# Loading v in rows of 16 KiB for sixteen heads at a time, and holding TensorE while both groups of stores are written

## The chip, the cores and the metric

The kernel runs on one core of a Trainium2 chip. The time is that of the whole execution on the device, in microseconds (us). A core has five engines that run side by side and wait for each other by semaphores: TensorE (PE; its weight loads are shown as PEld), VectorE (DVE), ScalarE (ACT), GpSimd (POOL) and SyncE (SP). Sixteen DMA engines move data between the memory outside (HBM) and the core's own memory (SBUF, 128 partitions); transfers are issued by POOL, by SP or by ACT, each with a queue of its own. TensorE writes its results to PSUM, eight banks of 2 KiB for each partition.

## The reference

```python
batch, n_heads, seq, head_dim = 8, 12, 1024, 64
# attn_weights: (8, 12, 1024, 1024) float32, v: (8, 12, 1024, 64) float32

def reference(attn_weights, v):
    return np.einsum('bhqs,bhsd->bhqd', attn_weights, v).astype(np.float32)
```

For each of 96 heads a matrix of 1024 x 1024 is multiplied by one of 1024 x 64. The weights are 403 MB, v and the result 25 MB each.

## The kernel before, in words

**Units.** Heads are taken four at a time, a quad; there are `NV` = 24 of them. A quad is worked in two units, so there are `NU` = 48, counted from 0 here. A partition of SBUF belongs to one of the four heads (32 partitions each) and has 32 rows of that head's weights; a unit has 16 of these rows for each partition. Its load (`load_attn`, L327) is issued by POOL and turns float32 into bfloat16 on the way: 8 MiB are read, 64 KiB in one piece for each partition, and 4 MiB are written to one of the two buffers `abf`. The last two units are loaded in two halves each.

**TensorE.** The loop at L212 has one turn for a quad, with `pe_unit` for each of its units. A unit waits for its load, and transposes it in 16 steps `g` of four matmuls (`transpose_g`, L134); pairs of bfloat16 values are moved as one float32 word. DVE and ACT copy the banks to `at` (L255). Ahead of step 8 TensorE waits for `s_half`, a semaphore that counts units. After the transposes, the first unit of a quad spreads v (`spread_v`, L149), both units transpose the products of the unit before back (`transpose_back`, L161; copied to `osb` by ACT, L238), and then multiply (`multiply`, L176; copied to `ot`, L267).

**v.** v arrives with 32 rows of a head in each partition (8 KiB of float32 in one piece), and is wanted with the rows at other places. `spread_v` does this by matmuls: for each of the four heads, `VB` = 4 matmuls of 32 partitions by 512 columns, with a matrix of ones and zeros (`spread`) as weights, summed in one bank. DVE and ACT copy the four banks to `vbf` (L231). Two quads are loaded together (`load_v`, L333, 2 MiB read), into `vr`, which has a place for each of the two; TensorE's branch at L197 picks the place. The load is issued by POOL when the odd quad of the two before has been spread (a wait for `s_sp`). The first two quads come by SP's queue as float32, in two loads (L124, and L396 in SP's list), to a part of `osb` not in use yet; DVE turns the first to bfloat16 (L312) and POOL the second (L382).

**Order on POOL and SP.** POOL goes through the units: for unit `n` the v load if one is due, then a wait for the last transposes of the unit (`s_t`), then the load of unit `n + 2`, and after units 16 and 32 the stores. Results are gathered in `osb` (ten places): quads 0 to 7 are stored in one DMA of 8 MiB, quads 8 to 15 in two of 2 and 6 MiB (`BURSTS`), the next four by POOL in two of 2 MiB after the last load, and the last four by SP. SP's list hands on semaphores: it waits for a v load and counts up `s_vr` for TensorE; it waits for the first two groups of stores and counts up `s_free` for ACT; it waits for the second halves of the last units and counts up `s_half` (L408). Before that, one increment at the start of the list sets `s_half` to `HALVED` = 46, so only the last two units wait in the middle.

Of the kernel before, what the change touches and what calls it, by code (L numbers as in the profile page):

```python
# [10 lines left out]
def kernel(  # L11
# [18 lines left out]
    nc = tc.nc  # L30
    fp32 = mybir.dt.float32
    bf16 = mybir.dt.bfloat16
    PE, DVE, ACT = (getattr(mybir.EngineType, x) for x in ("PE", "DVE", "Activation"))

    B, H, Q, S = attn_weights.shape
    D = v.shape[-1]
    NH = B * H
    P = 128
    VH = 4
    VP = P // VH  # L40
# [2 lines left out]
    HP = P // 2  # L43
    KW = S // (2 * P)
    SB = S // P
    VB = S // VP // SB
    NV = NH // VH
    NU = 2 * NV

# [1 line left out]
    HELD_FROM = NV - 8  # L51
# [2 lines left out]

    NO = 8 + 2
    V_SLOT = 4

    HALVED = NU - 2
    TOGETHER = 8
    BURSTS = {8: ((0, 8),), 16: ((8, 2), (10, 6))}  # L60

    def slot(q):
        return q % NO
# [5 lines left out]
    def out_n(q, fours):  # L69
# [1 line left out]
            "(n four) (p r) d -> (four p) n (r d)", four=VH, p=VP  # L71
        )

    v_2 = v.rearrange("b h q d -> (b h) q d").rearrange(
        "(hq two four) (p r) d -> hq (four p) two (r d)", two=2, four=VH, p=VP
    )

    def on_dve(g):
        return g % 8 in (0, 2, 4, 5, 7)
# [8 lines left out]
    sem = tc.alloc_semaphore  # L88
    sb = lambda name, shape, dt: nc.alloc_sbuf_tensor(name, shape, dt).ap()
    ident = sb("ident", [P, P], fp32)  # L90
    spread = sb("spread", [P, VB, P], bf16)
    abf = [sb(f"abf{i}", [P, G, S], bf16) for i in range(2)]
    at = sb("at", [P, G, KW, P, 2], bf16)
    vr = sb("vr", [P, 2, VB, SB * D], bf16)
    vbf = sb("vbf", [P, SB, VH, D], bf16)
    ot = sb("ot", [P, GH, P], fp32)
    osb = sb("osb", [P, NO, 2 * G, D], fp32)

    v32 = osb[:, ds(V_SLOT, 2)].rearrange("p n r d -> p n (r d)")
    bank = [nc.alloc_psum_tensor(f"bank{i}", [P, 512], fp32).ap() for i in range(8)]  # L100
    pt = [b.rearrange("p (k j) -> p k j", k=KW) for b in bank[:4]]
    po = bank[4:6]
    px = bank[6:8]
# [1 line left out]

    s_abf = [sem(f"s_abf{i}") for i in range(2)]
    s_second = {n: sem(f"s_second{n}") for n in range(HALVED, NU)}
    s_v0, s_v = sem("s_v0"), sem("s_v")
    s_osb = sem("s_osb")
    s_held, s_end = sem("s_held"), sem("s_end")  # L110

# [8 lines left out]
    s_const, s_vr = sem("s_const"), sem("s_vr")  # L120

    s_half, s_free = sem("s_half"), sem("s_free")

    nc.sync.dma_start(out=v32[:, 0], in_=v_2[0][:, 0])  # L124

    with tc.tile_critical(sync_engine=mybir.EngineType.Pool, no_gpsimd_drain=True):  # L126
        pe = nc.tensor

        def transpose_g(a, g, n):
            if g >= 4:  # L130
                pe.wait_ge(s_cp[g - 4], n)
            words = a[:, g].bitcast(fp32).rearrange("p (c k) -> p k c", k=KW)
            for k in range(KW):
                last = pe.matmul(  # L134
                    out=pt[g % 4][:, k],
                    lhsT=words[:, k],
                    rhs=ident,
                    is_transpose=True,
                    start=(k == 0),
                    stop=(k == KW - 1),  # L140
                )
            last.then_inc(s_t[on_dve(g)])

        def spread_v(two, banks):

            for h, ps in enumerate(banks):
                rows = ds(h * VP, VP)
                for b in range(VB):
                    last = pe.matmul(  # L149
                        out=ps,  # L150
                        lhsT=spread[rows, b],
                        rhs=vr[rows, two, b],
                        start=(b == 0),
                        stop=(b == VB - 1),
                    )
                last.then_inc(s_sp)

        def transpose_back(parts=((0, 4, px[0]), (4, 4, px[1]))):
            for j0, jn, ps in parts:
                for j in range(jn):  # L160
                    last = pe.matmul(  # L161
                        out=ps[:, ds(j * P, P)],
                        lhsT=ot[:, j0 + j],
                        rhs=ident,
                        is_transpose=True,
                        start=(j == 0),
                        stop=(j == jn - 1),
                    )
                last.then_inc(s_back)
# [16 lines left out]
        def pe_unit(i, n, both, loaded, it):  # L186

            pe.wait_ge(*loaded)
            for g in range(G):
                if g == GH:  # L190
                    pe.wait_ge(s_half, n)
                transpose_g(abf[i], g, n)
            pe.wait_ge(s_ot, both)
            if i == 0:
                pe.wait_ge(s_vr, it)
                odd = pe.snap((it - 1) % 2)
                with pe.If(odd > 0):  # L197
                    spread_v(1, po + px)
                with pe.Else():
                    spread_v(0, po + px)  # L200
                pe.wait_ge(s_vbf, it * 4)
            transpose_back()
            pe.wait_ge(s_last, both)
            for hp in range(2):
                for h in range(2):
                    for half in range(2):
                        outs = po[hp][ds(half * D, D), ds(h * GH * VP, GH * VP)]
                        last = multiply(outs, 2 * hp + h, half)
                last.then_inc(s_m)

        pe.wait_ge(s_const, 3 + VH)
        with nc.Fori(1, NV + 1, 1, engines=(PE,)) as it:  # L212
            loaded = pe.snap(it * 16)
            second = pe.snap(it * 2)
# [96 lines left out]
        for half in range(2):  # L311
            last = nc.vector.tensor_copy(  # L312
                out=vr[:, 0, ds(half * (VB // 2), VB // 2)].rearrange("p b x -> p (b x)"),
                in_=v32[:, 0, ds(half * (SB * D * VB // 2), SB * D * VB // 2)],
            )
        last.then_inc(s_vr)
        engine(True)
        engine(False)
        nc.scalar.wait_ge(s_held, 16 * (BY_SYNC - HELD_FROM) // 2)
# [2 lines left out]
        pool = nc.gpsimd  # L322

        def load_attn(n):
            pieces = [(0, G)] if n < HALVED else [(0, GH), (GH, GH)]
            for g0, gn in pieces:
                pool.dma_start(  # L327
                    out=abf[n % 2][:, ds(g0, gn)].rearrange("p g s -> p (g s)"),
                    in_=attn_q[n // 2][:, ds((n % 2 * G + g0) * S, gn * S)],
                ).then_inc(s_abf[n % 2] if g0 == 0 else s_second[n], 16)  # L330

        def load_v(iv):
            pool.dma_start(  # L333
                out=vr.rearrange("p two b x -> p two (b x)"), in_=v_2[iv]
            ).then_inc(s_v, 16)

        def store(q, fours, eng, done):
# [7 lines left out]
        def store_2(q):  # L345
# [7 lines left out]
            out=ident,  # L353
            in_=ident,
            compare_op=mybir.AluOpType.not_equal,
            fill=1.0,
            base=0,
            pattern=[[-1, P]],
            channel_multiplier=1,
        ).then_inc(s_const)  # L360

        for h in range(VH):
            pool.wait_ge(s_const, h + 3)
            pool.affine_select(  # L364
                out=spread[ds(h * VP, VP)],
                in_=spread[ds(h * VP, VP)],
                compare_op=mybir.AluOpType.not_equal,
                fill=1.0,
                base=0,
                pattern=[[1, VB], [-1, P]],  # L370
                channel_multiplier=VB,
            ).then_inc(s_const)
        for n in range(NU - 2):
            q, i = n // 2, n % 2
            if i == 0 and q % 2 == 1 and q + 1 < NV:
                pool.wait_ge(s_sp, 4 * (q + 1))
                load_v((q + 1) // 2)
            pool.wait_ge(s_t[True], (n + 1) * PER_DVE)
            load_attn(n + 2)
            if n == 0:  # L380
                pool.wait_ge(s_v0, 16)
                pool.tensor_copy(  # L382
                    out=vr[:, 1].rearrange("p b x -> p (b x)"), in_=v32[:, 1]
                ).then_inc(s_vr)
            if i == 0 and q % TOGETHER == 0 and 0 < q <= HELD_FROM:
                for q0, fours in BURSTS[q]:
                    store(q0, fours, pool, s_osb)
# [5 lines left out]

        nc.sync.dma_start(out=v32[:, 1], in_=v_2[0][:, 1]).then_inc(s_v0, 16)  # L396
        nc.sync.sem_inc(s_free, NO // 2)
        nc.sync.sem_inc(s_half, HALVED)
        for k in range(1, NV // 2):
            nc.sync.wait_ge(s_v, 16 * k)  # L400
            nc.sync.sem_inc(s_vr, 2)
            stored = 2 * (k - 1)
            if stored % TOGETHER == 0 and 0 < stored <= HELD_FROM:
                nc.sync.wait_ge(s_osb, 16 * sum(len(BURSTS[x]) for x in BURSTS if x <= stored))
                nc.sync.sem_inc(s_free, TOGETHER // 2)
        for n in range(HALVED, NU):
            nc.sync.wait_ge(s_second[n], 16)
            nc.sync.sem_inc(s_half)  # L408
        nc.sync.wait_ge(s_osb, 16 * sum(len(x) for x in BURSTS.values()))
        store(NV - 4, 2, nc.sync, s_end)  # L410
# [4 lines left out]
            out=out_q[NV - 1], in_=osb[:, slot(NV - 1)].rearrange("p r d -> p (r d)")  # L415
# [35 lines left out]
```

## Time and profile before

| What | us |
|---|---|
| median of 3 runs | 1052.8 (1052.76 to 1053.04) |
| the profiled execution | 1052.94 |
| its span, first to last instruction or landing | 1051.2 |
| TensorE busy / its weight loads | 731.1 / 686.2 |
| VectorE / ScalarE / GpSimd busy | 388.2 / 410.3 / 44.6 |
| transposes (L134), 3072 matmuls | 446.8 |
| spreading v (L149), 384 matmuls | 26.1 |
| attention loads, POOL, 46 of 4 MiB in SBUF: issue to landing, median | 30.9 |
| v loads, POOL, 11 of 1 MiB in SBUF: issue to landing, median | 12.5 |
| first v loads, SP, 2 of 1 MiB: issue to landing, median | 14.4 |

"Busy" is the time in which an engine had an instruction of its own under way. A DMA's time from issue to landing holds its stay in the queue behind other transfers. The profile divides the span into 40 slices and gives the busy share of each engine and of the DMA engines in tenths, so that a 9 is a slice that is full.

### The profile page before, as it was taken

To read this page: it belongs to the slowest core of one execution; us is meant where nothing else is said; L and a number is where in the kernel's file an instruction comes from. 1 tells how busy PE (TensorE), PEld (TensorE's weight loads), DVE (VectorE), ACT (ScalarE), POOL (GpSimd) and SP (SyncE) were. 2 spreads that over 40 slices of the span, in tenths; PEclk is the share of its full clock that TensorE was granted. 3 is DMA by queue.
4 is the path that set the end of the run, shared out by engine and by line. 5 is a ranking of instruction groups with operands and counts; after the bars stand their busy time and mean duration, and the time that the engine had idled before them with its cause. 6 is when DMAs were issued, how large, how long until landed. Compare 5 with 4: busy or idle time off the path is not lost.

```text
span 1051.2 us, 16374 instructions
## 1 busy us (share of the span) xinstructions
PE 731.1 (70%) x6920; PEld 686.2 (65%) x6920; DVE 388.2 (37%) x583; ACT 410.3 (39%) x493; POOL 44.6 (4%) x76
## 2 busy tenths in 40 slices
PE   0877688679579576457957858758716875875985
PEld 0767687578478575457857758658716865875874
DVE  1443344335335333233523434335303433532543
ACT  0444345335335333233533434335304433533543
POOL 2000000000000000000000000001000000000000
PEclk9989889889889898688989889889868988988898
DMA  9999999999999999999999999999999999999998
GB/s 233 227 220 217 218 218 208 216 219 219 219 217 218 216 207 379 219 219 217 217 216 208 219 219 219 207 229 217 359 225 219 219 206 229 218 206 218 218 218 343
DMA packets 13685, 240.19 MB, mean 228 GB/s; under 512 B 1136, under 2 KB 1136, under 8 KB 3952
## 3 DMA queue, kind: packets, MB, share of 16 engines
q0 software_dynamic: 12832, 233.84, 99.2%
q1 hardware_dynamic: 848, 6.29, 1.5%
q8 instruction: 2, 0.03, 0.0%
q14 instruction: 3, 0.02, 0.0%
HBM read 427.82 MB, written 25.17 MB: 431 GB/s over the span
## 4 chain that ended last, share of the span: by engine, by line
DMA 78%; PE 20%; issue 1%; POOL 0%; DVE 0%; ACT 0%; POOLq 0%; SPq 0%
DMA abf<-in_attn_weights_dram 78%; PE bank L134 20%; PE bank L176 0%; PE bank L161 0%; POOL abf L327 0%; DVE osb L238 0%; ACT ot L267 0%; SPq L408 0%; POOLq L435 0%; POOLq L126 0%
## 5 line engine op out<-in xcount | busy, mean ns | idle before, releaser
L134 PE MATMUL bank<-ident,abf 128*128 128x128 f32 x3072 | 446.8, 315 | 277.6 <-DMA abf<-in_attn_weights_dram 273.6
L134 PEld LDWEIGHTS bank<-ident,abf 128*128 128x128 f32 x3072 | 437.3, 214 | 290.4 <-DMA abf<-in_attn_weights_dram 285.8
L255 DVE COPY at<-bank 128x1024 bf16<-128x1024 bf16 x480 | 320.4, 689 | 486.8 <-PE bank L134 484.2
L255 ACT COPY at<-bank 128x1024 bf16<-128x1024 bf16 x288 | 288.8, 1012 | 411.9 <-PE bank L134 411.9
L176 PE MATMUL bank<-at,vbf 128*64 128x256 bf16 x3072 | 215.0, 278 | 0.0
L176 PEld LDWEIGHTS bank<-at,vbf 128*64 128x64 bf16 x3072 | 196.7, 108 | 13.4 <-DVE at L255 4.0
L267 ACT COPY ot<-bank 128x512 f32<-128x512 f32 x48 | 28.1, 586 | 174.0 <-PE bank L176 174.0
L267 DVE COPY ot<-bank 128x512 f32<-128x512 f32 x48 | 33.2, 692 | 151.4 <-PE bank L176 151.4
L161 PE MATMUL bank<-ident,ot 128*128 128x128 f32 x392 | 52.2, 276 | 32.5 <-DVE vbf L231 31.9
L161 PEld LDWEIGHTS bank<-ident,ot 128*128 128x128 f32 x392 | 43.4, 141 | 44.6 <-DVE vbf L231 43.7
L238 ACT COPY osb<-bank 128x512 f32 (+1 forms) x97 | 52.1, 589 | 27.3 <-PE bank L161 26.2
L327 POOL DMA_DIRECT2D abf<-in_attn_weights_dram x50 | 27.1, 542 | 716.9 <-PE bank L134 716.0
L231 DVE CAST vbf<-bank 128x512 bf16<-128x512 f32 x48 | 30.9, 686 | 6.5 <-PE bank L149 6.5
L231 ACT CAST vbf<-bank 128x512 bf16<-128x512 f32 x48 | 25.8, 589 | 11.8 <-PE bank L149 11.8
L149 PE MATMUL bank<-vr,spread 32*128 32x512 bf16 x384 | 26.1, 377 | 0.0
L255 ACT ACT_TABLE_LOAD x12 | 15.4, 1283 | 6.1 <-DMA osb<-in_v_dram 5.9
L333 POOL DMA_DIRECT2D vr<-in_v_dram x11 | 7.7, 703 | 228.7 <-PE bank L149 228.7
L149 PEld LDWEIGHTS bank<-vr,spread 32*128 32x128 bf16 x384 | 11.0, 92 | 6.2
L340 POOL DMA_DIRECT2D out_dram<-osb x5 | 3.9, 785 | 6.9 <-ACT osb L238 6.6
L364 POOL TENSOR_SCALAR_AFFINE_SELECT spread<-spread 32x512 bf16<-32x512 bf16 x4 | 3.6, 900 | 0.6
L306 DVE MEMSET ident<- 128x128 f32 x1 | 0.2, 165 | 5.9 <-DMA osb<-in_v_dram 5.9
L382 POOL CAST vr<-osb 128x2048 bf16<-128x2048 f32 x1 | 1.9, 1883 | 0.0
(9 smaller groups left out, 4.3 us busy)
## 6 DMA issues: line engine op xcount, KB each, us to landing
abf<-in_attn_weights_dram POOLq DMA_DIRECT2D x46, 4096.0 KB, 30.9
vr<-in_v_dram POOLq DMA_DIRECT2D x11, 1024.0 KB, 12.5
out_dram<-osb POOLq DMA_DIRECT2D x1, 8192.0 KB, 44.5
abf<-in_attn_weights_dram POOLq DMA_DIRECT2D x4, 2048.0 KB, 24.0
out_dram<-osb POOLq DMA_DIRECT2D x3, 2048.0 KB, 35.8
out_dram<-osb POOLq DMA_DIRECT2D x1, 6144.0 KB, 44.9
osb<-in_v_dram SPq DMA_DIRECT2D x2, 1024.0 KB, 14.4
out_dram<-osb SPq DMA_DIRECT2D x1, 2048.0 KB, 13.9
```

The source lines that it names most:

```text
L134: last = pe.matmul(out=pt[g % 4][:, k], lhsT=words[:, k], rhs=ident, is_transpose=True, start=(k == 0), stop=(k == KW - 1),)
L149: last = pe.matmul(out=ps, lhsT=spread[rows, b], rhs=vr[rows, two, b], start=(b == 0), stop=(b == VB - 1),)
L161: last = pe.matmul(out=ps[:, ds(j * P, P)], lhsT=ot[:, j0 + j], rhs=ident, is_transpose=True, start=(j == 0), stop=(j == jn - 1),)
L176: last = pe.matmul(out=outs, lhsT=vbf[:, 2 * kw + par, h], rhs=at[:, ds(half * GH, GH), kw, ds(h * VP, VP), par], start=(n == 0), stop=(n ...
L231: copy(out=vbf[:, :, h], in_=ps.rearrange("p (k d) -> p k d", k=SB)).then_inc(s_vbf)
L238: return copy(out=rows.rearrange("p (half j) d -> p j half d", half=2)[:, ds(j0, jn)], in_=ps[:, ds(0, jn * P)].rearrange("p (j half d) -> ...
L255: ins = copy(out=at[:, g].rearrange("c k j two -> c (k j two)"), in_=bank[g % 4].bitcast(bf16),)
L267: copy(out=ot.rearrange("c j (h p) -> c h j p", h=VH)[:, ds(2 * e, 2)], in_=po[e].rearrange("c (h j p) -> c h j p", h=2, j=GH),).then_inc( ...
L327: pool.dma_start(out=abf[n % 2][:, ds(g0, gn)].rearrange("p g s -> p (g s)"), in_=attn_q[n // 2][:, ds((n % 2 * G + g0) * S, gn * S)],).th ...
L333: pool.dma_start(out=vr.rearrange("p two b x -> p two (b x)"), in_=v_2[iv]).then_inc(s_v, 16)
L340: eng.dma_start(out=out_n(q, fours), in_=at_slot, **({"single_packet": True} if eng is pool and fours == 2 else {}),).then_inc(done, 16)
L364: pool.affine_select(out=spread[ds(h * VP, VP)], in_=spread[ds(h * VP, VP)], compare_op=mybir.AluOpType.not_equal, fill=1.0, base=0, patte ...
```

## The change

v comes in rows of 16 KiB: a partition holds 64 rows of a head, 16 partitions make a head, and 128 partitions hold eight heads, two quads. `V8` is 8, `VB` (matmuls for each head in `spread_v`) goes from 4 to 8. The two quads of such a load lie in the same place of `vr`, in other partitions; `vr` has two of these places, so four quads. After the first two quads (SP, one load), POOL loads quads 2 and 3 together, and then four quads at a time, at quads 4, 8, 12, 16 and 20 (`V_LOADS`). TensorE's branch picks one of four parts. A matmul of `spread_v` still takes 32 partitions, which now hold parts of two heads; `spread`, written by one select on POOL, has zeros where the other head lies. `spread` is 1080 elements for each partition in place of 512. The conversion of the first two quads is DVE's alone.

`s_half` starts at 18 in place of 46 and is counted up by 16 when the first store has landed and by 12 when both stores of the second group have: so units 18 and 34 wait for these in the middle of their transposes. In SP's list the wait for a group of stores comes ahead of that for a v load.

```diff
-    VB = S // VP // SB
+    V8 = 2 * VH
+    VB = S // (P // V8) // SB
+    VR = 32
...
+    V_AT_ONCE = 4
+    V_LOADS = {2: 2, **{q: V_AT_ONCE for q in range(V_AT_ONCE, NV, V_AT_ONCE)}}
...
+    ENDS = [2 * q + 2 for q in BURSTS] + [HALVED]
+    WHOLE = [n - m for m, n in zip([0] + ENDS, ENDS)]
...
-    v_2 = v.rearrange("b h q d -> (b h) q d").rearrange(
-        "(hq two four) (p r) d -> hq (four p) two (r d)", two=2, four=VH, p=VP
-    )
+    v_h = v.rearrange("b h q d -> (b h) q d")
+
+    def v_n(q, fours):
+        return v_h[ds(q * VH, fours * VH)].rearrange(
+            "(n eight) (p r) d -> (eight p) n (r d)", eight=V8, p=P // V8
+        )
...
-    spread = sb("spread", [P, VB, P], bf16)
+    spread = sb("spread", [P, V8, P + VB - 1], bf16)
...
-    vr = sb("vr", [P, 2, VB, SB * D], bf16)
+    vr = sb("vr", [P, V_AT_ONCE // 2, VB, SB * D], bf16)
...
-    nc.sync.dma_start(out=v32[:, 0], in_=v_2[0][:, 0])
+    nc.sync.dma_start(out=v32, in_=v_n(0, 2)[:, 0])
...
-        def spread_v(two, banks):
+        def spread_v(n, banks):
 
             for h, ps in enumerate(banks):
-                rows = ds(h * VP, VP)
+                j = n % 2 * VH + h
+                rows = ds(j * (P // V8) // VR * VR, VR)
                 for b in range(VB):
                     last = pe.matmul(
                         out=ps,
-                        lhsT=spread[rows, b],
-                        rhs=vr[rows, two, b],
+                        lhsT=spread[rows, j, ds(VB - 1 - b, P)],
+                        rhs=vr[rows, n // 2, b],
...
-                odd = pe.snap((it - 1) % 2)
-                with pe.If(odd > 0):
-                    spread_v(1, po + px)
+                which = pe.snap((it - 1) % V_AT_ONCE)
+                with pe.If(which > 1):
+                    with pe.If(which > 2):
+                        spread_v(3, po + px)
+                    with pe.Else():
+                        spread_v(2, po + px)
                 with pe.Else():
-                    spread_v(0, po + px)
+                    with pe.If(which > 0):
+                        spread_v(1, po + px)
+                    with pe.Else():
+                        spread_v(0, po + px)
...
-        pe.wait_ge(s_const, 3 + VH)
+        pe.wait_ge(s_const, 4)
...
-        def load_v(iv):
+        def load_v(q, fours):
             pool.dma_start(
-                out=vr.rearrange("p two b x -> p two (b x)"), in_=v_2[iv]
+                out=vr[:, ds(q % V_AT_ONCE // 2, fours // 2)].rearrange("p n b x -> p n (b x)"),
+                in_=v_n(q, fours),
             ).then_inc(s_v, 16)
...
-            if i == 0 and q % 2 == 1 and q + 1 < NV:
+            if i == 0 and q + 1 in V_LOADS:
                 pool.wait_ge(s_sp, 4 * (q + 1))
-                load_v((q + 1) // 2)
+                load_v(q + 1, V_LOADS[q + 1])
             pool.wait_ge(s_t[True], (n + 1) * PER_DVE)
             load_attn(n + 2)
-            if n == 0:
-                pool.wait_ge(s_v0, 16)
-                pool.tensor_copy(
-                    out=vr[:, 1].rearrange("p b x -> p (b x)"), in_=v32[:, 1]
-                ).then_inc(s_vr)
...
-        nc.sync.dma_start(out=v32[:, 1], in_=v_2[0][:, 1]).then_inc(s_v0, 16)
         nc.sync.sem_inc(s_free, NO // 2)
-        nc.sync.sem_inc(s_half, HALVED)
+        nc.sync.sem_inc(s_half, WHOLE[0])
         for k in range(1, NV // 2):
-            nc.sync.wait_ge(s_v, 16 * k)
-            nc.sync.sem_inc(s_vr, 2)
             stored = 2 * (k - 1)
-            if stored % TOGETHER == 0 and 0 < stored <= HELD_FROM:
+            if stored in BURSTS:
+                done = list(BURSTS).index(stored)
                 nc.sync.wait_ge(s_osb, 16 * sum(len(BURSTS[x]) for x in BURSTS if x <= stored))
                 nc.sync.sem_inc(s_free, TOGETHER // 2)
+                nc.sync.sem_inc(s_half, WHOLE[done + 1])
+            if 2 * k in V_LOADS:
+                nc.sync.wait_ge(s_v, 16 * (1 + list(V_LOADS).index(2 * k)))
+                nc.sync.sem_inc(s_vr, V_LOADS[2 * k])
```

More of the change, by code (lines that the diff above doesn't have):

```diff
@@ L97 @@
     osb = sb("osb", [P, NO, 2 * G, D], fp32)
-    v32 = osb[:, ds(V_SLOT, 2)].rearrange("p n r d -> p n (r d)")
+    v32 = osb[:, ds(V_SLOT, 2)].rearrange("p n r d -> p (n r d)")
     bank = [nc.alloc_psum_tensor(f"bank{i}", [P, 512], fp32).ap() for i in range(8)]
@@ L107 @@
     s_second = {n: sem(f"s_second{n}") for n in range(HALVED, NU)}
-    s_v0, s_v = sem("s_v0"), sem("s_v")
+    s_v = sem("s_v")
     s_osb = sem("s_osb")
@@ L313 @@
                 out=vr[:, 0, ds(half * (VB // 2), VB // 2)].rearrange("p b x -> p (b x)"),
-                in_=v32[:, 0, ds(half * (SB * D * VB // 2), SB * D * VB // 2)],
+                in_=v32[:, ds(half * (SB * D * VB // 2), SB * D * VB // 2)],
             )
-        last.then_inc(s_vr)
+        last.then_inc(s_vr, 2)
         engine(True)
@@ L360 @@
         ).then_inc(s_const)
[L362 to L372, printed above, removed]
+        pool.wait_ge(s_const, 3)
+        pool.affine_select(
+            out=spread,
+            in_=spread,
+            compare_op=mybir.AluOpType.not_equal,
+            fill=1.0,
+            base=VB - 1,
+            pattern=[[-P, V8], [-1, P + VB - 1]],
+            channel_multiplier=VB,
+        ).then_inc(s_const)
         for n in range(NU - 2):
             q, i = n // 2, n % 2
-            if i == 0 and q % 2 == 1 and q + 1 < NV:
+            if i == 0 and q + 1 in V_LOADS:
                 pool.wait_ge(s_sp, 4 * (q + 1))
-                load_v((q + 1) // 2)
+                load_v(q + 1, V_LOADS[q + 1])
             pool.wait_ge(s_t[True], (n + 1) * PER_DVE)
             load_attn(n + 2)
-            if n == 0:
-                pool.wait_ge(s_v0, 16)
-                pool.tensor_copy(
-                    out=vr[:, 1].rearrange("p b x -> p (b x)"), in_=v32[:, 1]
-                ).then_inc(s_vr)
             if i == 0 and q % TOGETHER == 0 and 0 < q <= HELD_FROM:
```

## The prediction

> **What bounds the kernel now.** I read the slices of the span first, then the DMA queues, the chain of waits and the timeline of TensorE.
>
> ```profile
> PE   0877688679579576457957858758716875875985
> DMA  9999999999999999999999999999999999999998
> q0 software_dynamic: 12832, 233.84, 99.2%
> ```
>
> The DMA row is full in every slice while TensorE's has holes: the sixteen DMA engines set the time. The chain of waits says the same, load after load:
>
> ```profile
> DMA 78%; PE 20%; issue 1%; POOL 0%; DVE 0%; ACT 0%; POOLq 0%; SPq 0%
> 303.97 28.84 DMA abf<-in_attn_weights_dram
> 332.81 0.04 issue
> 332.86 8.03 PE bank L134 x64
> 340.88 0.29 issue
> 341.18 35.21 DMA abf<-in_attn_weights_dram
> ```
>
> Its 20% of TensorE are no bound of their own: while a unit is transposed, the load of the next is under way (35.21 from issue to landing, of which the queue ahead is a good part). The timeline gives prices, because TensorE starts a unit when its load has landed:
>
> ```profile
> 212.02 9.43 PE L134 MATMUL bank<-ident,abf 128*128 128x128 f32 x64 [2.08 <-DMA abf<-in_attn_weights_dram]
> 231.34 10.41 PE L134 MATMUL bank<-ident,abf 128*128 128x128 f32 x64 [4.61 <-DMA abf<-in_attn_weights_dram]
> 250.70 8.02 PE L134 MATMUL bank<-ident,abf 128*128 128x128 f32 x64 [1.10 <-DMA abf<-in_attn_weights_dram]
> 274.88 9.28 PE L134 MATMUL bank<-ident,abf 128*128 128x128 f32 x64 [10.88 <-DMA abf<-in_attn_weights_dram]
> 395.73 10.17 PE L134 MATMUL bank<-ident,abf 128*128 128x128 f32 x64 [4.53 <-DMA abf<-in_attn_weights_dram]
> 434.62 9.63 PE L134 MATMUL bank<-ident,abf 128*128 128x128 f32 x64 [20.88 <-DMA abf<-in_attn_weights_dram]
> ```
>
> Third column: idle before. Landings of plain loads lie 19.32 us apart (231.34 - 212.02), so 8.389 MB move at 434 GB/s. A v load between two makes it 24.18 (274.88 - 250.70), so v costs 4.86; the 8 MiB store makes it 38.89 (434.62 - 395.73), so it costs 19.57.
>
> **The change, part by part.** The sum is made against the profiled execution's 1052.94 us (span 1051.2); the median of the runs is 1052.8, 0.1 lower.
>
> *Rows of v.* One v load is 2.097 MB; at the 434 GB/s of the loads, whose rows are 64 KiB, that is 4.83 us. It costs 4.86, so shorter rows and one more DMA together cost 0.03 to 0.06 (another pair, 332.86 to 357.07, gives 4.89). Eleven loads: 0.3 to 0.7 us. That is all there is to win. Rows twice as long halve the rows' part, and six loads for eleven take away five of eleven DMAs' parts: -0.4 taken, ends 0 and -0.7. A second way of pricing is a rival below.
> The Trainium skill, "DMA: Bandwidth & Descriptors", section on the anatomy of one DMA, has about 2.0 us fixed for each DMA; by it five DMAs less would be an estimated 10 us. The 4.86 above speaks against paying that in a full queue.
>
> *TensorE held.* From unit 18 (start 395.73) the second half of the transposes waits for the first store, from unit 34 for the other two. The store ends where load 19 begins, 434.62 - 19.32 = 415.3. Then 32 transposes, at the half clock that follows such idle time, take 5.6 (as at 1010.60 below), and load 20 goes out near 421.5, before at 408.03. Load 19 is still under way until 434.3, which hides 12.8 us. Behind the held transposes stand only this unit's spread, product and copies; they end near 421.0 + 6.2 + 1.35 + 1.09 + 4.48 = 434.1 (spread as below), when load 19 lands. The second group lies alike. Cost nothing; without that cover 13.5 each. SP waits for the stores ahead of the v loads of later quads: nothing of those is due. For the stores themselves I see no gain: 8.389 MB in 19.57 is the loads' rate already, with TensorE at work beside.
>
> *Start.* SP's one load of 2 MiB replaces two of 1 MiB. DVE, ACT and POOL start with the first's landing, at 5.89. The two took 4.8 (its own view) and, from the median 14.4 of both, 24.0 us; the second ran beside attention's load 0. So the new one lands between 8.3 (2.4 us more bytes) and 29.8; I take 18. DVE then needs 0.17 + 0.57 (a memset of 540 words for 256 in 0.27) before POOL's selects, 0.28 and, at 0.90 per 512 elements, 1.9 for 1080 in one; the casts are 4 of 0.87 instead of 2. All is ready near 24, before load 0 lands at 27.11. At 29.8 TensorE would start 5.6 late (29.8 + 0.17 + 0.57 + 0.28 + 1.9), load 2 would go out at 43.2 for 37.57, and load 1 lands only at 47.66. Nothing either way. POOL's cast (1.88) leaves.
>
> *The spread (L149).*
>
> ```profile
> 323.76 1.07 PE L149 MATMUL bank<-vr,spread 32*128 32x512 bf16 x16
> 325.27 0.70 POOL L333 DMA_DIRECT2D vr<-in_v_dram  x1 [20.77 <-PE bank L149]
> 325.97 0.56 POOL L327 DMA_DIRECT2D abf<-in_attn_weights_dram  x1
> 332.86 1.35 PE L134 MATMUL bank<-ident,abf 128*128 128x128 f32 x9 [1.17 <-DMA abf<-in_attn_weights_dram]
> ```
>
> Sixteen of mean 377 ns end in 1.07 us: four chains side by side, one per group of 32 partitions; in the records matmuls of one group start 0.216 apart. After, it is 32 matmuls, and two heads share a group, so a quad uses two groups, sixteen in each. Two full chains side by side: 15 x 0.216 + 0.38 = 3.6; all in line: 7.1. In L176's records the second half of the columns starts with the fifth matmul of the first half, so about four wait for one part of the array; then the second group starts with the thirteenth of the first: 12 x 0.216 + 3.6 = 6.2. I take 6.2, 5.1 later than now.
> The Trainium skill, "TensorE: Matmul & The Clock Gate", rules for kernel authors, wants each small-K matmul in its own row group and has 3.07 times for four; giving up half of the groups for twice the matmuls is against it: estimated 4 x 1.07 = 4.3 us by its pattern, with the sum as it is.
> Who waits? DVE's and ACT's casts, TensorE's own rest, and in six units POOL: its v load, and the load queued behind it, go out after the spread. The load in flight then lands 7.59 later (332.86 - 325.27); 2.5 remain. Pairs of units take TensorE 9.4 + 6.2 + 1.35 + 1.09 + 4.48 and 9.4 + 1.09 + 4.5 + 0.4 = 37.9, the DMA 38.64 and its share of v: still DMA's. Where it now idles 4.61 its clock halves for a while (10.41 against 8.02); less idle time gives some of it back. Cost in the steady part: nothing as forecast.
>
> *End.*
>
> ```profile
> 1010.60 5.59 PE L134 MATMUL bank<-ident,abf 128*128 128x128 f32 x32 [2.04 <-SPq L408]
> 1016.13 1.07 PE L149 MATMUL bank<-vr,spread 32*128 32x512 bf16 x16
> 1023.97 4.14 PE L134 MATMUL bank<-ident,abf 128*128 128x128 f32 x32
> 1029.98 4.14 PE L134 MATMUL bank<-ident,abf 128*128 128x128 f32 x32 [1.87 <-SPq L408]
> 1041.93 0.33 SPq L414 DMA_DIRECT2D out_dram<-osb  x1
> ```
>
> The last bank is copied 4.6 later, so 1023.97 becomes 1028.6 and the last transposes 1032.7, 2.7 late; the last store goes out at 1044.6. In the DMA view of the end the engines stay full to 1047.4 with the stores queued since 1000.55 and 1030.05; 2.4 us of that is the last store, so it must be there by 1045.0. SP's first packets come 1.0 after issue (0.74, 1.75): 1045.6. Between 0 and +0.6; +0.2 taken, as the engines run out over 2 us.
>
> Sum: -0.4 + 0 + 0 + 0 + 0.2 = -0.2 to 1052.7, or 1052.6 beside the median.
>
> **The rivals.**
> *The queue runs dry behind v (slower).* Six times POOL issues v with 2.5 us left. From POOL's issue to the first packet the trace bounds the time only at the start: load 0, issued at 1.34, has none before 4.7 (only SP's queue moves until then), at most 3.4; SP's row gives 1.0. At 3.4 each v load costs 0.9, with a spread of 7.1 it costs 1.8: 5.4 to 10.8; where the clock stays full instead of 10.41, 2.4 come back, which saves about half of the places: 3 us, 1055.8. It decides where the spread's delay and the first packet's delay together exceed 7.6. For it: an unseen delay with a wide bound. Against: SP's shorter row, and engines that end a load up to 1 us apart.
> *Longer rows win more (faster).* By packets alone: the records have 324 ns for a row of 8 KiB and 2432 for 64 KiB, a fixed 23 ns a row; eight rows fewer per engine and eight heads make 12 x 8 x 0.023 = 2.2: 1050.7. Against it: records overlap (the queue row exceeds 100% in steady windows), and landings, which do not, show 0.06.
> *Each DMA pays its start in the full queue (faster).* The rows bound a start between 1.0 and 3.4 (above); five less win 5 to 17, about 1042. Against it: 4.86 for a whole v load leaves no room. The page on DMA named above says as much with its 2.0.
> *TensorE becomes the bound.* If the spread ran in line and at half clock, 14 us, a pair would need 45.7 against 41.1 with v: 24 x 4.6 = 110, 1163. Only if the clock fell in the midst of work, which no row shows.
>
> **How the numbers follow.** Forecast 0.66; queue dry 0.22; longer rows 0.06, starts paid 0.02; TensorE 0.02; 0.02 unseen. A measurement can tell 0.2%, 2.1 us, from no change: 1050.7 to 1054.9 is "same". The forecast's own range is 1052.0 to 1053.5. Forecast and a quarter of the dry case are same: 0.72; slower 0.2; faster 0.08. The range 1050.6 to 1056.5 takes in the rows' rival and the dry case at its middle.
>
> **What would show it.** Right: landings 19.32 apart; around a v load of sixteen heads 29.0 (4 MiB, 9.7); L149 x32 in about 6 us; no hole in the DMA row. Held units show their second half near 415. The dry rival shows idle DMA after each v issue and a landing gap over 29.3. Wrong: any gap between landings that bytes at 434 GB/s do not fill, or a last store that ends well after the others.

## The result, and the profile after

The changed kernel takes 1062.36 us (median of 5 runs, 1061.03 to 1064.43) against 1052.8 before; the ratio is 1.0092, with a 95% interval from 1.0081 to 1.0104. It is 9.6 us slower, where 0.2 less was forecast and 1050.6 to 1056.5 was the range. The profiled execution took 1061.98, its span is 1060.2 (before 1051.2).

The page of the changed kernel: busy shares, the slices of the span, the DMA queues and the chain that ended last.

```profile
PE 895.9 (84%) x7304; PEld 739.1 (70%) x7304; DVE 391.6 (37%) x583; ACT 413.3 (39%) x493; POOL 37.8 (4%) x67
PE   0998799599999594989959999959578995999997
DMA  9999999999999999999999999999999999999997
q0 software_dynamic: 11344, 233.84, 98.6%
DMA 53%; PE 44%; ACT 1%; issue 1%; POOL 0%; DVE 0%; ACTq 0%; SPq 0%; POOLq 0%
L159 PE MATMUL bank<-vr,spread 32*128 32x512 bf16 x768 | 181.5, 426 | 0.5 <-issue 0.2
L186 PE MATMUL bank<-at,vbf 128*64 128x256 bf16 x3072 | 248.2, 304 | 0.0
```

The bytes are the same. TensorE's busy time went from 731.1 to 895.9, and of that 155 is the spread of v (26.1 to 181.5). TensorE has 44% of the chain, before 20%: the DMA engines still look full in every slice, but they no longer set the time everywhere. The multiplications are slower too (304 ns for 278 each) though nothing in them was changed: the chain below has 6.29 for a unit's 64 behind a slow spread, at a granted clock of 0.67, and 4.41 for the next unit's, at 1.00.

Stretches of the same kernel, one spread in each: time, busy time, granted clock, DMA share, GB/s.

```profile
75.60:81.90 6.30, 6.30 (x33) 0.97 0.92 198
283.50:293.00 9.50, 9.46 (x33) 0.65 0.98 210
859.00:867.50 8.50, 8.23 (x33) 0.74 0.90 193
```

At full clock a spread takes 6.3. But in the second and third TensorE is busy without a gap until the spread ends (the third stretch runs 0.3 longer), and the clock still falls to half in their midst; then they take 8.2 to 9.5.

The chain of waits, one pair of units and the next in a stretch with no v load due (start, us, what):

```profile
623.87 7.95 PE bank L143 x64
631.82 9.49 PE bank L159 x32
641.31 0.02 issue
641.34 0.59 ACT vbf L247
641.93 0.04 issue
641.97 1.97 PE bank L171 x8
643.94 6.29 PE bank L186 x64
650.24 7.88 PE bank L143 x64
658.12 0.88 PE bank L171 x8
658.99 4.41 PE bank L186 x64
663.40 7.88 PE bank L143 x64
671.29 8.03 PE bank L159 x32
679.32 0.28 issue
679.60 0.70 POOL vr L349
680.30 32.62 DMA abf<-in_attn_weights_dram
```

There is no wait for a load in it: from 623.87 to 663.40 the pair takes 39.53, where two loads take 38.64. TensorE falls behind the DMA, the next spread ends at 679.3, and POOL issues v only at 679.60. By the trace's records of DMA packets the load ahead of it ends, on the mean of the sixteen engines, at 680.79; the first packet of v starts at 681.00, 1.40 after its issue, and v ends, on the same mean, 10.82 after the load ahead of it, where 9.71 is the undisturbed time (experiment 1). At 867.53 the same happens with 0.5 us left: first packet 868.93, again 1.40, and 1.66 us lost.

The end, in the chain:

```profile
1022.93 8.09 PE bank L159 x32
...
1031.68 1.97 PE bank L171 x8
1033.65 6.01 PE bank L186 x64
1039.66 7.88 PE bank L143 x64
...
1054.64 0.69 DVE osb L254
```

By the packet records the last load is in at 1036.3 (before 1029.6), but TensorE is still at the unit before and takes up the last one at 1039.66. The DMA view of the last 12 us, in slices of 0.3 us, shows what that does:

```profile
DMA  9999999999998321000000000049999999700000
1055.36 0.33 SPq L427 DMA_DIRECT2D out_dram<-osb  x1
```

The engines have written all other stores by 1053 and stand idle until the last store, issued at 1055.36, arrives. So of 9.0 us more of span, 6.7 lie ahead of the last landing and 2.3 behind it.

### The profile page after: what moved, and what is told of

The parts are those of the page before. It is cut to its first block, busy times and chain, and to the rows that moved or that the text cites. A ratio compares the mean times of both kernels' runs of the same rounds, so it can differ in the third digit from the quotient of the medians.

```text
span 1060.2 us, 17156 instructions
## 1 busy us (share of the span) xinstructions
PE 895.9 (84%) x7304; PEld 739.1 (70%) x7304; DVE 391.6 (37%) x583; ACT 413.3 (39%) x493; POOL 37.8 (4%) x67
## 3 DMA queue, kind: packets, MB, share of 16 engines
q1 hardware_dynamic: 704, 6.29, 1.5%
## 4 chain that ended last, share of the span: by engine, by line
DMA 53%; PE 44%; ACT 1%; issue 1%; POOL 0%; DVE 0%; ACTq 0%; SPq 0%; POOLq 0%
DMA abf<-in_attn_weights_dram 46%; PE bank L143 24%; PE bank L159 11%; DMA out_dram<-osb 7%; PE bank L186 7%; PE bank L171 2%; ACT vbf L247 1%; POOL vr L349 0%; ACT osb L254 0%; ACT at L271 0%; ACT L271 0%; DVE osb L254 0%; ACT ot L283 0%; ACTq L254 0%; ACTq L304 0%
## 5 line engine op out<-in xcount | busy, mean ns | idle before, releaser
L143 PE MATMUL bank<-ident,abf 128*128 128x128 f32 x3072 | 403.5, 295 | 141.3 <-DMA abf<-in_attn_weights_dram 110.0
L143 PEld LDWEIGHTS bank<-ident,abf 128*128 128x128 f32 x3072 | 393.8, 210 | 152.5 <-DMA abf<-in_attn_weights_dram 115.0
L186 PE MATMUL bank<-at,vbf 128*64 128x256 bf16 x3072 | 248.2, 304 | 0.0
L186 PEld LDWEIGHTS bank<-at,vbf 128*64 128x64 bf16 x3072 | 218.6, 119 | 28.5 <-issue 7.9
L159 PE MATMUL bank<-vr,spread 32*128 32x512 bf16 x768 | 181.5, 426 | 0.5 <-issue 0.2
L159 PEld LDWEIGHTS bank<-vr,spread 32*128 32x128 bf16 x768 | 68.3, 101 | 96.1 <-issue 31.4
L171 PE MATMUL bank<-ident,ot 128*128 128x128 f32 x392 | 73.2, 349 | 16.9 <-ACT vbf L247 16.2
L171 PEld LDWEIGHTS bank<-ident,ot 128*128 128x128 f32 x392 | 60.5, 182 | 38.1 <-ACT vbf L247 37.2
L271 ACT ACT_TABLE_LOAD x12 | 15.4, 1283 | 18.9 <-DMA osb<-in_v_dram 18.7
L349 POOL DMA_DIRECT2D vr<-in_v_dram x6 | 4.1, 677 | 120.4 <-PE bank L159 120.4
L322 DVE MEMSET ident<- 128x128 f32 x1 | 0.2, 165 | 18.7 <-DMA osb<-in_v_dram 18.7
L328 DVE CAST vr<-osb 128x2048 bf16<-128x2048 f32 x2 | 3.3, 1672 | 0.0
```

What stands on the lines that cost most here:

```text
L143: last = pe.matmul(out=pt[g % 4][:, k], lhsT=words[:, k], rhs=ident, is_transpose=True, start=(k == 0), stop=(k == KW - 1),)
L159: last = pe.matmul(out=ps, lhsT=spread[rows, j, ds(VB - 1 - b, P)], rhs=vr[rows, n // 2, b], start=(b == 0), stop=(b == VB - 1),)
L171: last = pe.matmul(out=ps[:, ds(j * P, P)], lhsT=ot[:, j0 + j], rhs=ident, is_transpose=True, start=(j == 0), stop=(j == jn - 1),)
L186: last = pe.matmul(out=outs, lhsT=vbf[:, 2 * kw + par, h], rhs=at[:, ds(half * GH, GH), kw, ds(h * VP, VP), par], start=(n == 0), stop=(n ...
L271: ins = copy(out=at[:, g].rearrange("c k j two -> c (k j two)"), in_=bank[g % 4].bitcast(bf16),)
L328: last = nc.vector.tensor_copy(out=vr[:, 0, ds(half * (VB // 2), VB // 2)].rearrange("p b x -> p (b x)"), in_=v32[:, ds(half * (SB * D * V ...
```

## The experiments

Each ran beside the kernel before, on the same chip; ratios are to that (its medians were 1052.86 to 1052.96). The theory, A: the spread stands in line in one group of 32 partitions, the clock falls in it, and TensorE's loads go out late. Against it: B, the spread's length alone does it; C, the holding does it; D, v in pieces of 4 MiB does it.

**1. Two groups by turns.** Only the order of the spread's matmuls is changed (and the counts that the copies wait for):

```diff
-            for h, ps in enumerate(banks):
-                ...
-                for b in range(VB):
-                    last = pe.matmul(out=ps, ...)
-                last.then_inc(s_sp)
+            for pair in ((0, 2), (1, 3)):
+                for b in range(VB):
+                    for h in pair:
+                        last = pe.matmul(out=banks[h], ...)
+                        if b == VB - 1:
+                            last.then_inc(s_sp)
```

> The changed kernel with the spread's 32 matmuls in another order: heads 0 and 2 by turns, then 1 and 3, so that two groups of 32 partitions work side by side all the time. Theory A (the spread stands in line in one group, most of the array idle, the granted clock falls in its midst, TensorE reaches the DMA's pace and its loads go out too late): the spread takes about 3.6 us instead of 6.3 to 9.5, the landings lie 19.3 apart again, the last transposes start near 1030, and the time is 1052.0 to 1053.0. Rival C (holding TensorE for the stores costs the time): it stays at 1062. Rival D (v in pieces of 4 MiB costs the time in the DMA queue): it stays at 1062.

Measured: 1052.15 (1051.85 to 1052.55), ratio 0.9992 [0.9983, 1.0001]. The page and TensorE's timeline (start, us):

```profile
DMA 71%; PE 26%; issue 1%; POOL 0%; ACT 0%; DVE 0%; ACTq 0%; SPq 0%; POOLq 0%
L160 PE MATMUL bank<-vr,spread 32*128 32x512 bf16 x768 | 87.0, 375 | 0.5 <-issue 0.2
324.19 3.63 PE L160 MATMUL bank<-vr,spread 32*128 32x512 bf16 x32
```

The same 768 matmuls now take 87.0 in place of 181.5; every one of the 24 spreads takes 3.62 or 3.63. The whole loss is gone with the order of the matmuls alone. So neither v in pieces of 4 MiB nor the holding costs it. The sixteen-head loads land 9.71 behind the load ahead (9.80 once): two of the old ones are 9.80.

**2. No holding.**

```diff
-        nc.sync.sem_inc(s_half, WHOLE[0])
+        nc.sync.sem_inc(s_half, HALVED)
...
-                nc.sync.sem_inc(s_half, WHOLE[done + 1])
```

> The changed kernel with the semaphore for the second halves set to 46 at the start, as before: TensorE isn't held for the stores. Theory A and rival D: 1061 to 1064, as the changed kernel, perhaps 1 less where the held unit made the next late. Rival C: 1052 to 1054.

Measured: 1065.43 (1063.66 to 1066.74), ratio 1.0116 [1.0100, 1.0131]. The holding is not the cause. The time is 1.4 above what theory A gave. The 3.1 us more than the changed kernel are not shown to be the holding's merit: the intervals overlap (the changed kernel's is 1.0081 to 1.0104), and in this profile the v load of unit 2 is issued at 85.40 (82.20 in the changed kernel), before any unit is held, and costs 2.5 there.

**3. The holding alone**, in the kernel before:

```diff
-        nc.sync.sem_inc(s_half, HALVED)
+        nc.sync.sem_inc(s_half, WHOLE[0])
...
-            nc.sync.wait_ge(s_v, 16 * k)
-            nc.sync.sem_inc(s_vr, 2)
...
+                nc.sync.sem_inc(s_half, WHOLE[1 + list(BURSTS).index(stored)])
+            nc.sync.wait_ge(s_v, 16 * k)
+            nc.sync.sem_inc(s_vr, 2)
```

> The kernel before, with TensorE held in units 18 and 34 until the stores have landed, and SP's wait for the stores ahead of that for v; nothing else of the change. Theory A: 1052.6 to 1053.2, no change, since the load after the held unit still goes out 10 us before the queue needs it. Rival C: 1055 to 1062.

Measured: 1052.33 (1052.18 to 1052.56), ratio 0.9994 [0.9985, 1.0003]: no change that can be told. The median is 0.6 below the 1052.94 beside it, a little outside what was expected, but so it is in experiments 1, 7 and 9, with the holding and without.

**4. A long spread with the whole array at work**, in the kernel before:

```diff
-            for h, ps in enumerate(banks):
...
+            for again in range(7):
                 for b in range(VB):
...
+                    for h, ps in enumerate(banks):
...
```

> The kernel before, with each matmul of the spread done seven times (each repeat starts its sum anew) and the four groups of 32 partitions by turns: 28 in each group, about 6.2 us for a spread, with all four groups at work. It tells the length of the spread from the idle part of the array. Theory A: the granted clock stays up in the spread, it takes 6.2 in every unit, and the time is 1052.8 to 1054, with the last transposes some 3 us late. Rival B (a spread 5 us longer is enough, by POOL's v load issued late and TensorE's turn being full): 1059 to 1063. Rivals C and D: 1052.8.

Measured: 1063.72 (1062.01 to 1065.81), ratio 1.0097 [1.0081, 1.0112]. Theory A is wrong here and rival B right (0.7 above its range): length alone is enough to run the queue dry. What is left of A is a question of how much the clock adds, which the next experiment answers. The clock did stay up in 23 of the 24 spreads, as the stretch of one shows (in the first, TensorE stood still for 4.05 in its midst and went on at half clock), and the timeline has the v load behind it:

```profile
244.90:251.10 6.20, 6.19 (x113) 2.73 (x112) 0.69 (x1) 0.60 (x1) 0.00 (x0) 1.00 1.08 233
251.48 0.70 POOL L335 DMA_DIRECT2D vr<-in_v_dram  x1 [22.45 <-PE bank L150]
```

Eleven v loads stand behind such spreads; by the packet records nine of them lost 0.5 to 1.6 each, 7.7 in all. This one was issued 1.4 ahead of the end of the load in flight (252.86 by the packet records) and cost 1.5. The last load lands 13.5 late; behind it nothing is lost.

**5. A long spread in line**, in the kernel before:

```diff
             for h, ps in enumerate(banks):
                 rows = ds(h * VP, VP)
-                for b in range(VB):
+                for again in range(4 if h < 2 else 1):
+                    for b in range(VB):
...
```

> The kernel before, with the matmuls of heads 0 and 1 of each quad done four times (each repeat starts its sum anew): sixteen in line in one group of 32 partitions, sixteen in the next, then the other two heads with four each, as long and as idle as the spread of the changed kernel; v's rows, loads and the stores as before. Theory A: spreads of 6.2 to 9.5, the clock falls in them, 1060 to 1065, as the changed kernel (eleven v loads wait behind a spread here, six there, so it may be a little more). Rivals C and D: 1052.8.

Measured: 1071.78 (1067.09 to 1074.45), ratio 1.0187 [1.0172, 1.0203]. Where the clock holds a spread takes 6.26, as in experiment 4, but the kernel takes 8.1 more than that one, and is 6.8 above theory A's range. One spread, as a stretch and in the timeline, with the v load behind it:

```profile
325.70:335.10 9.40, 9.40 (x41) 3.31 (x40) 1.38 (x2) 0.60 (x1) 0.00 (x0) 0.65 0.94 202
325.67 9.50 PE L150 MATMUL bank<-vr,spread 32*128 32x512 bf16 x40
335.59 0.70 POOL L334 DMA_DIRECT2D vr<-in_v_dram  x1 [22.26 <-PE bank L150]
```

TensorE is busy throughout in both, with 113 matmuls at clock 1.00 or 41 at 0.65. So the falling clock goes with the idle part of the array, and it is a cost of its own on top of the length. The change of the rows, the loads and the holding are not in this kernel.

**6. v issued early**, with the changed kernel's slow spread:

```diff
-    V_LOADS = {2: 2, **{q: V_AT_ONCE for q in range(V_AT_ONCE, NV, V_AT_ONCE)}}
+    V_LOADS = {q: 2 for q in range(2, NV, 2)}
...
-                pool.wait_ge(s_sp, 4 * (q + 1))
+                pool.wait_ge(s_sp, 4 * (q - 1))
```

> The changed kernel with v loaded for two quads at a time, rows still 16 KiB, into the half of its place that isn't in use, so that POOL's v load waits for a spread two quads back and never for the one just done. The spread is as slow as in the changed kernel. It tells the share of the v issue from that of TensorE's own pace. If the queue runs dry behind v alone (the rival of the prediction as it was put): 1053 to 1054. Theory A, in which TensorE's pace and the late end are most of it: the two holes of about 1.1 and 1.7 us ahead of v loads go, the rest stays, 1057 to 1061.

Measured: 1057.48 (1056.93 to 1059.2), ratio 1.0041 [1.0026, 1.0057]. POOL's v load no longer waits for the spread just done, and 4.9 of the 9.6 us are back: the v loads cost nothing extra, the last load lands at 1031.7. Most of the rest is the end, in the profiled execution, the slowest of the four (1059.2): its span is 6.2 longer than before, 4.1 of that behind the last load and 2.1 ahead of its end, where by the packet records plain loads lost time. Its chain at the end:

```profile
1020.03 9.35 PE bank L159 x32
...
1036.91 7.88 PE bank L143 x64
```

TensorE reaches the last unit 5.2 after its load; the span ends 25.7 behind that landing, before 21.6.

**7. Both**: two groups by turns, and v issued early.

> Both: the spread with two groups by turns, and v for two quads at a time, not waiting for the spread just done. Theory A: 1052.2 to 1052.9; against the kernel before at most 0.5 us to win, since a v load's rows and its own DMA cost 0.03 to 0.06 us there.

Measured: 1052.16 (1052.03 to 1052.62), ratio 0.9993 [0.9984, 1.0002], as experiment 1.

**8. Two groups by turns in part three of the branch alone**:

```diff
+            if n == 3:
+                for pair in ((0, 2), (1, 3)):
+                    ...
+            else:
+                for h, ps in enumerate(banks):
+                    ...
```

> The changed kernel with two groups by turns in part three of TensorE's branch alone (quads 3, 7, 11, 15, 19 and 23, behind which five of the six v loads stand, and the last quad); the other eighteen spreads stay as slow as in the changed kernel. If the time is lost where POOL's v load waits and at the end (the experiments so far: 4.9 us by the v loads' issue, the rest behind the last load): 1052.3 to 1054. If TensorE's pace in all units is what costs: 1058 to 1062.

Measured: 1054.58 (1052.89 to 1057.27), ratio 1.0016 [1.0006, 1.0026]. It is 0.6 above the first range and gives back 7.8 of the 9.6 us: a slow spread costs most where a v load waits for it and at the end. A short spread in every fourth quad also lets TensorE catch up; the run does not tell that from the v load's wait. The 1.7 left, and the wide spread of its runs, are what the other eighteen spreads cost, the one ahead of the first v load among them.

**9. Two groups by turns, no holding.**

> The kernel with two groups by turns in all parts, without the holding of TensorE. With the queue full at all times the holding does nothing: 1052.0 to 1052.6, as with it (1052.15). If the holding itself wins time: about 1053.

Measured: 1052.3 (1052.01 to 1052.68), ratio 0.9995 [0.9986, 1.0005]; with the holding 0.9992. It does nothing.

**10. Experiment 4 with the holding.**

> The kernel before with spreads of 6.2 us in four groups (each matmul done seven times, each repeat starts its sum anew), as run before at 1063.7, and with TensorE held for both groups of stores. If holding helps when the queue is close to dry (the changed kernel without it took 3.1 us more, though part of that arose before the first hold): 1059 to 1062. If it doesn't: 1062 to 1066.

Measured: 1066.21 (1060.99 to 1070.31), ratio 1.0123 [1.0083, 1.0162], against 1.0097 without it. The intervals overlap; no help is seen where the queue is nearly dry.

No version beats the kernel before by more than the interval: the best, 0.9992 [0.9983, 1.0001], is not told from it.

## Why the prediction was wrong

*Rows of v* (forecast -0.4, bounds 0 and -0.7): right. In experiment 1 a load of sixteen heads ends 9.71 behind the load ahead for two of 4.90, and there are five of them (one of 9.80): with the one of eight heads (4.87), -0.4. Experiment 6, with the longer rows and eleven loads, has 4.87 to 4.89 for each. The rival of longer rows, -2.2, and that of starts paid, -5 or more, are refuted.

*The holding* (nothing): right, by experiments 3 and 9. The second half of unit 18 starts at 420.95, not near 415: v for eight heads more lies ahead of the store by then (experiment 3, with v as before, has 415.47). The load behind the held unit still goes out 12.5 us ahead (427.61 for 440.14, by landing), the cover that was forecast (12.8).

*The start* (v at 18, nothing lost): nearly right. DVE starts at 18.7, the first transposes at 27.95 in place of 27.11, load 2 goes out at 38.66, far ahead of load 1's landing; by the packet records load 3 ends 0.25 later than before, in experiment 1 too.

*The spread* (6.2, because two groups work one after the other): its mechanism was right. In the records the second group starts 2.61 us after the first, with its thirteenth matmul, and at full clock the 32 take 6.3. The Trainium skill, "TensorE: Matmul & The Clock Gate", section "Why this matters for your kernels", wants each small-K matmul in a row group of its own, so that they run side by side: the trace agrees, 3.63 with two groups side by side against 6.3.

*The step that failed* is the one that followed: "Pairs of units take TensorE 9.4 + 6.2 + 1.35 + 1.09 + 4.48 and 9.4 + 1.09 + 4.5 + 0.4 = 37.9, the DMA 38.64 and its share of v: still DMA's", with "less idle time gives some of it back. Cost in the steady part: nothing as forecast". Less idle time did shorten the transposes (7.95 for 9.4). But the clock fell in the spread itself, which then took up to 9.55, and the transposes back behind it ran at half clock (1.97 for 1.09), as did part of the multiplications (6.3 for 4.48): 39.53 for a pair against the DMA's 38.64. The text had the fall of the clock "in the midst of work" only as a rival at 0.02, "which no row shows"; no row of before could, as its spreads had four groups at work and took 1.07. The other support of "nothing" was that 2.5 us left at a v load's issue are enough. Experiment 4, where the clock held, shows that they are not: with 2.2 to 2.8 left a v load lost 0.5 to 0.8. How the 9.6 us divide between the spread's length and the fall of the clock in the changed kernel itself no run shows.

*The first rival*, the queue dry behind v, came true. It had 0.22, and the 2.5 us that remain, against a first packet after 1.0 to 3.4, were read as enough. Four of the six v loads had 3.1 to 3.7 left and lost 0.04 to 0.25 each; two, with the clock down, had 1.2 and 0.5 and lost 1.1 and 1.7. Over the kernels, by the packet records (the end of a load is the mean over the sixteen engines; a load of eight heads loses what goes beyond 4.90 behind the load ahead, one of sixteen what goes beyond 9.71):

| v issued ahead of the end of the load in flight, us | lost at this load, us |
|---|---|
| 6.1 and more (before) | 0.0 |
| 3.6 to 5.0 (experiment 1) | 0.0 to 0.1 |
| 3.1 to 3.7 (changed kernel) | 0.04 to 0.25 |
| 2.2 to 2.8 (experiment 4) | 0.5 to 0.8 |
| 1.4 to 2.0 (experiment 4) | 0.8 to 1.6 |
| 0.4 and 0.0 (experiment 5) | 1.9 and 2.4 |

So about 3 us are needed, and the limit is not sharp: one v load with 2.4 left lost 0.1 (experiment 5), one with 3.3 left 0.5 (experiment 10). In the changed kernel it is 1.4 to the first packet, and the first packets of the two late loads are slow (most took 0.7 to 1.3 us for 0.6). The price of the whole rival, 3 us, came near the v loads' own loss (3.2) by luck: it took 0.9 to 1.8 at each load from a first packet after 3.4, with half of the places saved, where two loads bear 2.8. Two plain loads issued 3.2 and 1.7 ahead lost 0.9 more, the last half load 0.9, and load 34, the one ahead of the second group of stores, 1.4: its packets took 3.3 to 4.1 us for 2.4 near 747, though it had been issued 7.6 ahead. What slowed these last two is open; other kernels with the long spread show it at such loads too (1.1 in experiment 4), the kernel before doesn't, and no run was made for it.

*The end* (+0.2, bounds 0 and +0.6): the mechanism was right and the size wrong. The last unit's transposes, both halves in one go, start at 1039.66 and so end near 1047.5, where the second half was forecast from 1032.7 to 1036.8: units 45 and 46 were late already, and the last spread took 8.1 at the lower clock. The last store is issued at 1055.36, not 1044.6, and the engines stand idle: 2.3.

## What to carry to other kernels

Matmuls of 32 partitions were dear twice here when they came group by group: heads that share a group of 32 partitions stood in line, and the granted clock fell while they did. When rows for a DMA are made longer, look first at what that does to the groups; here the order of the matmuls was worth 10 us and the rows 0.4. And where an engine issues a transfer behind another engine's work, count what is left in the queue at that moment: in these kernels a v load lost 0.5 us at most with more than 3 us left, and 0.7 to 1.6 with 1.4 to 2.0 left.

## What was not expected of the hardware

The granted clock fell to half while TensorE was busy without a gap, in spreads with one group of 32 partitions at work most of the time (0.65 over 9.4 us in experiment 5); with four groups by turns it stayed at 1.00 (6.2 us, experiment 4, in the 23 spreads without a gap), and with two, spreads of 3.63 were never lengthened. A v load issued by POOL to a queue about to run dry had its first packet 1.40 us later, twice to the hundredth in the changed kernel, and 1.40 to 1.50 in experiment 4 with 2.0 us or less left.
